# A decoder trunk with three token mixers: four Delta solutions planned side by side, with other ranks, waits, costs and priorities

## The chip, the core and the metric

The kernel runs on one core of a Trainium2 chip. The metric is the time of one execution on the device, in microseconds (us); of several runs the median counts. Four engines compute: TensorE (PE in the profile) multiplies matrices, VectorE (DVE) and ScalarE (ACT) work element by element, GpSimd (POOL) as well, and it also issues some of the transfers here; SyncE (SP) issues the others. Each engine works through its own queue in order and waits there for what its next instruction needs.

## What is computed

Two layers on 512 positions of width 1024. Each has one wide projection, three mixers side by side whose outputs are gated and merged, and a SwiGLU network:

```
for layer in range(DEPTH):
    h = rmsnorm(x, attn_norm[layer])
    proj = h @ w_in[layer]
    u_a, v_a, q_b, k_b, v_b, qkv_c, z_c, beta_c, a_c, gate_pre = split_columns(proj)
    out_a = spatial_gating(gelu(u_a), gelu(v_a), ...)
    out_b = sliding_window_attention(q_b, k_b, v_b, ...)
    out_c = gated_deltanet(qkv_c, z_c, beta_c, a_c, ...)
    merged = sum_i sigmoid(gate_i) * (out_i @ w_branch[layer, i])
    x = x + merged @ w_out[layer]
    gu = rmsnorm(x, ffn_norm[layer]) @ w_gate_up[layer]
    x = x + (silu(gu[..., :D_FF]) * gu[..., D_FF:]) @ w_down[layer]
return rmsnorm(x, final_norm)
```

The change concerns the gated DeltaNet, `out_c`, of four heads of width 128. Its core, in each chunk:

```
decay = exp(where(tril, gc[..., :, None] - gc[..., None, :], -inf))
lower = where(strict, (k_beta @ k^T) * decay, 0)
sol   = triangular_solve(lower + eye, [v * beta, k_beta * exp(gc)])
attn  = (q @ k^T) * decay
# then over the chunks, in order, with a state of 128 x 128 per head:
v_new = u_c - w_c @ state;  o_c = q_dec @ state + attn @ v_new
state = state * c_dec + k_dec^T @ v_new
```

## The kernel before

**Dense work.** All large products are made of 128x512 matmuls in three passes, each operand split into a high and a low part (`hH`, `hL`; `wh`, `wl`). A block of weights is loaded to `st`, rounded by ACT to `wh`, and DVE makes the rest `wl`; both carry a high priority. These matmuls write to four banks called `mm`.

**The Delta mixer.** The four heads form two groups (`Delta(gi)`) of two heads, and the 512 positions four chunks of 128 (`NCH`), so there are eight pairs of group and chunk. For each pair stand these steps, which share four banks called `px`: `decay` (a product of `gg`, the decays' logs, with a triangle; ACT's exponential; POOL's mask, into `la`), `keys` (transposes and squares of the keys, their norms on ACT and DVE, then `la[:, :, 0]`, written to memory as `blkscr`), `queries`, `values`, `solve` and `scan`. Once the keys of both groups are there, `blocks` inverts all diagonal blocks of 16x16 at once: POOL reads `blkscr` back as `nx`, DVE makes `tb` in 15 pairs of a product (`prd`) and a sum, POOL writes `tb` and its transpose to memory (`sc`) and reads them back as `cols`. Every `solve(c)` begins with `Tm` (DVE) and `Uc` (POOL) made from `cols`, and doubles the size of the block from 16 to 32, 64 and 128: PE makes a product, DVE or ACT evicts it as `ys`, PE makes the second, DVE subtracts it and transposes. `scan` goes through a group's chunks in order.

**The order of the work.** PE's order is fixed by a planner written by hand, `Issue`. Every stretch of work is a generator (a stream) with a rank, given by `spawn(rank, gen, after, slack)`. `run` takes the first ready stream in rank order up to its next `yield`; a lower rank goes first, and the dense work, rank 10 (`DENSE`), fills in when no other is due. A stream that yields a name waits until `set` of that name; one that yields a number is due at that time; a bare `yield` makes it due when all that it has just issued is done by the planner's reckoning (`issue.last`). `note` reckons these times with costs written in it, a latency `LAT` and so forth; they set PE's order only and are no times of the chip. On the other engines the framework's scheduler sets the order by its own reckoning and by the priorities given in the code (`tc.high_priority`).

The streams of a layer are these:

```
for e in d:
    issue.spawn(2, dn_stream(e))
    issue.spawn(3, e.solves())
    issue.spawn(1, qv_stream(e))
issue.spawn(4, keys_done())
```

Here `dn_stream` is decay and then keys, `qv_stream` queries, values and scan, `keys_done` blocks. Ranks 5 to 9 hold attention, the spatial gating and the branches' projections. The norm's stream has rank 0: `norm.finish()` starts from the time of its sums and a slack, 4.0 in layer 0, with four matmuls of `ones` and `sq` (the sums of squares), from which `rst`, the rows' scales, are made. `kv_out` then scales the keys and values of attention and the logits of beta and decay (`ba`), makes `gg` in a chain of small operations, and has PE sum it (`ex`).

The functions that the change touches and those that call them stand here with the line numbers of the profile (nearly all instructions are recorded under line 118, where the planner issues them, so they go by the names of their tiles):

Of the kernel before, what the change touches and what calls it, by code (L numbers as in the profile page):

```python
# [10 lines left out]
F32 = mybir.dt.float32  # L11
# [25 lines left out]
LAT = 0.7  # L37
DMA_LAT = 2.5
DENSE = 10
PAD = 48  # L40
ORDER = "k z qv0 qv1 aq gv u"
# [7 lines left out]
class Issue:  # L49
# [6 lines left out]
    def __init__(self):  # L56
        self.now = 0.0
        self.busy = {"vector": 0.0, "scalar": 0.0, "gpsimd": 0.0, "sync": 0.0}
        self.ready = {}
        self.read = {}  # L60
        self.banks = {}
        self.last = 0.0
        self.ahead = False
        self.events = {}
        self.streams = []

    def note(self, eng, op, args, kw):
        aps = [a for a in (*args, *kw.values()) if hasattr(a, "shape")]
        n = int(np.prod(aps[0].shape[1:]))
        dep = max((self.ready.get(a.tensor.name, 0.0) for a in aps), default=0.0)  # L70
        if eng == "tensor":
            m = int(np.prod(aps[1].shape[1:]))
            cost = n / 2400 if aps[1].dtype == F32R or op == "transpose" else max(4 * n, 4 * m) / 2400
            self.now = max(self.now, dep) + max(cost, m / 1200)
# [5 lines left out]
        else:  # L80
            if eng == "gpsimd":
                cost = 0.4 + n / 200 if ALU.pow in args else 0.1 + n / (430 if op == "tensor_tensor" else 900)
            else:
                cost = 0.07 + n / 960
            self.busy[eng] = max(self.busy[eng], self.now) + cost
            end = max(self.busy[eng], dep + cost) + LAT
# [4 lines left out]
        for a in [aps[0]] + ([kw["accum_out"]] if "accum_out" in kw else []):  # L91
            self.ready[a.tensor.name] = end
        self.last = max(self.last, end)
# [41 lines left out]
    def run(self):  # L135
        while self.streams:
# [12 lines left out]
            assert first is not None, [s[4] for s in self.streams]  # L149
            self.now = max(self.now, first[3])  # L150
# [12 lines left out]
def hybrid_kernel(ctx, tc, x0, pos, wi, wkv, wb, wo, wg, wd, gn, convw, lngb, sguw, sgub,  # L163
# [263 lines left out]
    def layer(l, norm, first=None):  # L427
        norm.after = f"kv{l}"
        issue.spawn(0, norm.finish(), norm.accs[0], 4.0 if l == 0 else 0.0)
# [35 lines left out]

        def kv_out():
# [3 lines left out]
            for c in range(NCH):  # L470
                r = rst[:, c:c + 1]
                nc.scalar.activation(kraw[:, c, :], banks[c][:, 0:128], AF.Copy, scale=r)
                nc.scalar.activation(vt[:, c, :], banks[c][:, 128:256], AF.Copy, scale=r)
                nc.vector.tensor_scalar(ba[:, c, :], banks[c][:, 256:264], r, None, ALU.mult)
            issue.set(f"kv{l}")
            nc.vector.tensor_scalar(rst8, rst, 0.125, None, ALU.mult)
            nc.vector.tensor_scalar(rsth, rst, 0.5, None, ALU.mult)

            def v44(t):
                return t.rearrange("p (c h) -> p c h", h=4)  # L480

            nc.vector.tensor_scalar(v44(bet), ba[:, :, 0:4], -1.0, 80.0, ALU.mult, ALU.min)
            nc.scalar.activation(bet, bet, AF.Exp)
            nc.vector.tensor_scalar(bet, bet, 1.0, None, ALU.add)
            nc.vector.reciprocal(bet, bet)
            sx = small("sx")
            nc.vector.tensor_tensor(v44(sx), ba[:, :, 4:8], db.unsqueeze(1).broadcast_to([P, NCH, 4]), ALU.add)
            se = small("se")
            nc.vector.scalar_tensor_tensor(se, sx, -1.0, sx, ALU.mult, ALU.min)
            nc.scalar.activation(se, se, AF.Exp)  # L490
            sz = small("sz")
            nc.vector.tensor_scalar(sz, se, 2.0, None, ALU.add)
            nc.vector.reciprocal(sz, sz)
            nc.vector.tensor_tensor(sz, sz, se, ALU.mult)
            sz2 = small("sz2")
            nc.vector.tensor_tensor(sz2, sz, sz, ALU.mult)
            spl = small("spl")
            nc.vector.tensor_scalar(spl, sz2, 1.0 / 17, None, ALU.mult)
            for kk in (15, 13, 11, 9, 7, 5, 3):
                nc.vector.scalar_tensor_tensor(spl, spl, 1.0 / kk, sz2, ALU.add, ALU.mult)  # L500

            nc.vector.scalar_tensor_tensor(spl, spl, 1.0, sz, ALU.add, ALU.mult)
            nc.vector.tensor_scalar(sx, sx, 0.0, None, ALU.max)
            nc.vector.scalar_tensor_tensor(spl, spl, 2.0, sx, ALU.mult, ALU.add)
            ea = small("ea", 4)
            nc.scalar.activation(ea, al, AF.Exp)
            nc.vector.tensor_scalar(ea, ea, -1.0, None, ALU.mult)
            nc.vector.tensor_tensor(v44(gg), v44(spl), ea.unsqueeze(1).broadcast_to([P, NCH, 4]), ALU.mult)
# [4 lines left out]
            nc.scalar.activation(ex, pgs[:, :48], AF.Exp)  # L513
            nc.vector.tensor_scalar(negc, egc, -1.0, None, ALU.mult)
# [36 lines left out]

        class Delta:
# [16 lines left out]
            def decay(self):  # L569

                for c in range(NCH):
                    col = self.col(c)
                    lg = self.wt([P, 2, P], "Tm", 2)
# [3 lines left out]
                    yield  # L577
# [4 lines left out]
                    nc.scalar.activation(la[:, :, 1, :], h2(ps), AF.Exp)  # L582
                    nc.gpsimd.tensor_tensor(la[:, :, 1, :], la[:, :, 1, :], bc(tri_le), ALU.mult)
                    self.la.append(la)
                    yield

            def keys(self):
# [4 lines left out]
                for c in range(NCH):  # L592
# [119 lines left out]
            def solves(self):  # L712
                for c in range(NCH):
                    if c >= 3:
                        yield f"o{l}{self.gi}{c - 3}"
# [656 lines left out]
```

## Time and profile before

| what | us |
|---|---|
| runs | 1751.05, 1754.48, 1752.0 |
| median | 1752.0 |
| the profiled execution | 1753.96 |
| its span, from the first to the last instruction | 1752.2 |
| PE busy / DVE / ACT / POOL | 1723.8 / 879.9 / 639.7 / 409.4 |

The mean granted clock of TensorE was 0.997 of its full rate. The profile names tiles as out<-in, so "mm<-hH,wh" is a dense matmul, "px<-Tm,la" the first product of a solution, "px<-ones,sq" one of the norm. Busy times of PE are modelled at the ends of the matmuls, so the distance from start to start tells more of its pace than the length of one. Mixers of layer 0 lie at some 30 to 300 us, those of layer 1 at some 900 to 1150 us; what lies between and after is the dense work of the branches and of the network.

### The profile page before, as it was taken

Reading aid. Unit: us, or ns where it says so; the run is one execution under the profiler, and the core shown is the slowest. Engines: PE = TensorE matmul, PEld = TensorE weight load, DVE = VectorE, ACT = ScalarE, POOL = GpSimd, SP = SyncE. Lnnn points to the kernel's source line nnn. Section 1 sums busy time; section 2 is a strip of 40 time slices with the busy share of each in tenths; the row PEclk is TensorE's granted clock in tenths of the full one; section 3 lists DMA queues with packets and bytes.
Section 4 is the critical chain, followed back from the end, with each engine's and each line's share of the span. In section 5 each row is a group of like instructions: output and inputs, shape, how many; then the busy total and the mean of one; then the engine's idle time right before and its main releaser. Section 6 shows DMA issues by size and latency. Waiting matters only on the chain.

```text
span 1752.2 us, 22016 instructions
## 1 busy us (share of the span) xinstructions
PE 1723.8 (98%) x8324; PEld 1424.9 (81%) x8324; DVE 879.9 (50%) x1744; ACT 639.7 (37%) x1180; POOL 409.4 (23%) x447
## 2 busy tenths in 40 slices
PE   9999899999999999999999999999999999999998
PEld 8888678888888888888888877788888888888886
DVE  7695775444543333323266958654445433333224
ACT  6454643322333222222244545533233322222212
POOL 2423221011223333310024142210212233333000
PEclk9999999999999999999999999999999999999999
DMA  5232102222352222234332220122223534444222
GB/s 165 87 106 85 37 25 90 85 93 100 102 181 96 97 96 97 96 107 134 121 121 87 97 73 25 55 85 97 96 86 131 162 120 121 120 121 156 97 97 84
DMA packets 73114, 176.57 MB, mean 101 GB/s; under 512 B 24944, under 2 KB 25200, under 8 KB 73008
## 3 DMA queue, kind: packets, MB, share of 16 engines
q1 hardware_dynamic: 71184, 170.71, 30.1%
q0 software_dynamic: 1248, 3.41, 0.7%
q8 instruction: 65, 1.06, 0.3%
q10 hardware_dynamic: 576, 1.05, 0.2%
q14 instruction: 41, 0.34, 0.1%
HBM read 162.03 MB, written 13.11 MB: 100 GB/s over the span
## 4 chain that ended last, share of the span: by engine, by line
PE 92%; DVE 4%; ACT 2%; POOL 1%; issue 1%; DMA 0%; SPq 0%; POOLq 0%; ACTq 0%; DVEq 0%
PE mm L118 81%; PE px L118 11%; ACT pr L118 1%; DVE pr L118 1%; DVE wl L118 0%; DVE U L118 0%; DVE zg L118 0%; POOL of L118 0%; DVE gw L118 0%; DMA x<-in_x 0%; ACT wh L118 0%; DVE gv L118 0%; DVE Tm L118 0%; DVE xf L118 0%; DVE ys L118 0%
## 5 line engine op out<-in xcount | busy, mean ns | idle before, releaser
L118 ACT CAST wh<-st 128x1024 fp32r<-128x1024 f32 (+2 forms) x286 | 295.9, 1035 | 829.5 <-PE mm L118 627.0
L118 PE MATMUL mm<-hH,wh 128*128 128x512 f32 x1344 | 532.5, 396 | 0.0
L118 PE MATMUL mm<-hH,wl 128*128 128x512 f32 x1344 | 523.8, 390 | 0.0
L118 PE MATMUL mm<-hL,wh 128*128 128x512 f32 x1344 | 523.2, 389 | 0.0
L118 DVE TENSOR_TENSOR wl<-st,wh 128x1024 fp32r<-128x1024 f32 (+2 forms) x286 | 352.5, 1232 | 222.1 <-ACT wh L118 211.4
L118 PEld LDWEIGHTS mm<-hH,wl 128*128 128x128 f32 x1344 | 252.2, 188 | 53.6
L118 PEld LDWEIGHTS mm<-hH,wh 128*128 128x128 f32 x1344 | 252.4, 188 | 53.3 <-issue 3.5
L118 PEld LDWEIGHTS mm<-hL,wh 128*128 128x128 f32 x1344 | 252.6, 188 | 50.9 <-issue 1.2
L118 POOL TENSOR_TENSOR s<-s,rep 128x512 f32<-128x512 f32 x44 | 77.6, 1763 | 162.0 <-ACT s L118 162.0
L118 POOL TENSOR_TENSOR aL<-s,aH 128x512 fp32r<-128x512 f32 x44 | 77.5, 1761 | 156.5 <-ACT aH L118 156.5
L118 POOL TENSOR_TENSOR gt<-gt,gt 128x512 f32<-128x512 f32 x32 | 48.8, 1524 | 272.6 <-DVE gt L118 272.6
L118 DVE TENSOR_TENSOR s<-mm,s 128x512 f32<-128x512 f32 x44 | 30.4, 692 | 143.9 <-PE mm L118 137.1
L118 DVE TENSOR_TENSOR s<-mm,rep 128x512 f32<-128x512 f32 x44 | 30.4, 691 | 138.3 <-PE mm L118 114.6
L118 DVE TENSOR_TENSOR gt<-mm,rep 128x512 f32<-128x512 f32 x48 | 33.1, 690 | 105.6 <-PE mm L118 105.6
L118 PE MATMUL mm<-wh,hH 128*128 128x512 f32 (+1 forms) x208 | 84.3, 406 | 1.2 <-ACT hH L118 1.2
L118 PE MATMUL mm<-wh,hL 128*128 128x512 f32 (+1 forms) x208 | 80.2, 385 | 0.6 <-DVE hL L118 0.6
L118 PE MATMUL mm<-wl,hH 128*128 128x512 f32 (+1 forms) x208 | 79.8, 384 | 0.0
L118 PE MATMUL mm<-brH,wh 128*128 128x512 f32 x192 | 74.7, 389 | 0.0
L118 PE MATMUL mm<-brL,wh 128*128 128x512 f32 x192 | 74.7, 389 | 0.0
L118 PE MATMUL mm<-brH,wl 128*128 128x512 f32 x192 | 74.7, 389 | 0.0
L118 PE MATMUL mm<-aH,wh 128*128 128x512 f32 x176 | 68.5, 389 | 0.0
L118 PE MATMUL mm<-aL,wh 128*128 128x512 f32 x176 | 68.5, 389 | 0.0
(285 smaller groups left out, 2510.9 us busy)
## 6 DMA issues: line engine op xcount, KB each, us to landing
st<-in_wi SPq DMA_DIRECT2D x104, 512.0 KB, 3.2
st<-in_wg SPq DMA_DIRECT2D x88, 512.0 KB, 3.3
st<-in_wb SPq DMA_DIRECT2D x24, 512.0 KB, 3.2
st<-in_wt SPq DMA_DIRECT2D x22, 512.0 KB, 3.2
st<-in_wo SPq DMA_DIRECT2D x16, 512.0 KB, 3.2
st<-in_wd SPq DMA_DIRECT2D x16, 512.0 KB, 3.6
xscr<-xt SPq DMA_DIRECT2D x24, 256.0 KB, 2.0
xt<-xscr SPq DMA_DIRECT2D x24, 256.0 KB, 2.9
```

The costliest lines, as they stand in the source:

```text
L118: return f(*args, **kw)
```

## The change

No instruction is added or removed; order, waits, priorities and buffers change.

- Planner: `LAT` 0.7 to 0.5; other costs in `note`, with the cost of a change between whole and partial tiles on PE; within `soon()` a result is reckoned from PE's own time.
- `soon()`, new: sets `issue.first` and a priority of 200 for what it encloses: the decays' exponential and mask, the keys' small operations and `la`, all of `blocks`, the evictions of `solve` and of the scan's states.
- `kv_out`: its operations stand under a high priority, in another order (the four on `ba` first, the chain of `gg` ahead of most else, ACT's scaling in the middle); `ea` is made ahead of it.
- Steps of decays, keys, queries and values yield `issue.bank_free("px", 4)` and `issue.now`: they wait for a free bank, no longer for their own last result.
- `solves(i)`: two streams per group, each with every second chunk; the wait of chunk 3 for the group's first output is gone. `scan` is a stream of its own; queries and values have rank 4.
- Buffers: `Tm`, `ys`, `Uc` 2 to 4 each, `U` 6 to 8. The norm's slack in layer 0: 4.0 to 1.0. The memory of the descriptors of dynamic transfers: set to 8192.

```diff
-LAT = 0.7
+LAT = 0.5
+SOON = 200
...
+                cost = (4 * max(n, m) + 24) / (4800 if tiled else 2400)
+            if tiled != self.tiled:
+                cost += 0.09
...
-            end = max(self.busy[eng], dep + cost) + LAT
+            end = max(self.now + cost, dep + cost) + 0.3 if self.first else max(self.busy[eng], dep + cost)
+            end += LAT
...
-        issue.spawn(0, norm.finish(), norm.accs[0], 4.0 if l == 0 else 0.0)
+        issue.spawn(0, norm.finish(), norm.accs[0], 1.0 if l == 0 else 0.0)
...
+        @contextmanager
+        def soon():
+            issue.first = True
+            with tc.high_priority(SOON):
+                yield
+            issue.first = False
...
-                    lg = self.wt([P, 2, P], "Tm", 2)
+                    lg = self.wt([P, 2, P], "Tm", 4)
...
-                    yield
+                    yield max(issue.last, issue.bank_free("px", 4))
...
                 for c in range(NCH):
+                    yield issue.bank_free("px", 4)
...
-                    yield
+                    yield issue.now
...
-                Tm, U = wt([P, 2, P], "Tm", 2), wt([P, 2, P], "Uc", 2)
+                with soon():
+                    Tm, U = wt([P, 2, P], "Tm", 4), wt([P, 2, P], "Uc", 4)
...
-            def solves(self):
-                for c in range(NCH):
-                    if c >= 3:
-                        yield f"o{l}{self.gi}{c - 3}"
-                    yield f"blocks{l}"
+            def solves(self, i):
+                yield f"blocks{l}"
+                for c in range(i, NCH, 2):
                     yield from self.solve(c)
 
             def scan(self):
                 yield f"z{l}"
+                yield f"qv{l}{self.gi}"
...
-            yield from e.scan()
+            issue.set(f"qv{l}{e.gi}")
...
             issue.spawn(2, dn_stream(e))
-            issue.spawn(3, e.solves())
-            issue.spawn(1, qv_stream(e))
+            for i in range(2):
+                issue.spawn(3 + i / 10, e.solves(i))
+            issue.spawn(4, qv_stream(e))
+            issue.spawn(1, e.scan())
...
-    nc = bacc.Bacc("TRN2", target_bir_lowering=False, num_devices=1)
+    nc = bacc.Bacc("TRN2", target_bir_lowering=False, num_devices=1, dynamic_dma_scratch_size=8192)
```

Three places of the order. First PE at the head of layer 0, where the norm's sums are multiplied (`px<-ones,sq`). Before, they stand among dense matmuls of the first wide tile (`mm_69`):

```order
L118 MATMUL mm_69_371<-hH_22_138,wh_71_373 128x512
L118 MATMUL mm_69_371<-hL_23_139,wh_71_373 128x512
L118 MATMUL mm_69_371<-hH_22_138,wl_72_374 128x512
L118 MATMUL px_73_399<-ones_78,sq_26_188 128x1 x4
L118 MATMUL mm_69_371<-hH_24_142,wh_71_373 128x512
L118 MATMUL mm_69_371<-hL_25_143,wh_71_373 128x512
```

In the change they stand inside the matmuls of 264 columns (`px_46`, `px_47`: keys and values of attention):

```order
L137 MATMUL px_46_246<-wh_16_117,hH_20_130 128x264
L137 MATMUL px_46_246<-wl_17_118,hH_20_130 128x264
L137 MATMUL px_46_246<-wh_16_117,hL_21_131 128x264
L137 MATMUL px_48_314<-ones_78,sq_26_188 128x1 x4
L137 MATMUL px_47_247<-wh_16_117,hH_18_126 128x264
L137 MATMUL px_47_247<-wl_17_118,hH_18_126 128x264
```

The norm's matmuls moved ahead, in front of the last tile of the narrow projection.

Second PE at the first solutions of layer 0 (`px<-Tm,la` is a solution's first product, `px<-ys,Uc` its second, `px<-kT,qT` attention). Before:

```order
L118 MATMUL mm_1681<-wl_1720,hH_112 128x512
L118 MATMUL mm_1681<-wh_1719,hL_113 128x512
L118 MATMUL px_1763<-Tm_1743,la_664 128x128 x2
L118 MATMUL px_1768<-Tm_1747,la_670 128x128 x2
L118 MATMUL px_1779<-kT_1220,qT_1741 128x128
L118 MATMUL px_1780<-kT_1220,qT_1741 128x128
...
L118 MATMUL px_1817<-ys_1766,Uc_1744 128x128 x2
L118 MATMUL px_1824<-ys_1771,Uc_1748 128x128 x2
```

In the change (`px<-dq,dk` are steps of queries):

```order
L137 MATMUL mm_1210<-hL_139,wh_1212 128x512
L137 MATMUL mm_1210<-hH_138,wl_1213 128x512
...
L137 MATMUL px_1266<-dq_1029,dk_384 128x128
L137 MATMUL px_1266<-dq_1120,dk_462 128x128
L137 MATMUL px_1278<-Tm_1235,la_535 128x128 x2
L137 MATMUL px_1283<-Tm_1239,la_547 128x128 x2
L137 MATMUL px_1288<-Tm_1243,la_562 128x128 x2
L137 MATMUL px_1293<-Tm_1247,la_574 128x128 x2
L137 MATMUL px_1298<-ys_1281,Uc_1236 128x128 x2
```

Four solutions, two of each group, now start together, and without attention between; in the program they come some 280 rows sooner on PE.

Third DVE at the end of `blocks` in layer 0 (`prd` and `tb` are its product and sum, `COPY` its transpose). Before:

```order
L118 TENSOR_REDUCE tb_1399<-prd_1402 128x14
L118 TENSOR_TENSOR prd_1402<-tb_1399,nx_1396 128x225
L118 TENSOR_REDUCE tb_1399<-prd_1402 128x15
L118 TENSOR_TENSOR wl_1684<-st_1682,wh_1683 128x1024
L118 COPY nx_1396<-tb_1399 128x256
L118 TENSOR_TENSOR Tm_1743<-cols_1434,blk_155 128x256
```

In the change (`pre`, `cv`, `dq` are steps of a convolution; `mm_1162` is the last tile of the first group's values):

```order
L137 TENSOR_REDUCE tb_903<-prd_906 128x14
L137 SCALAR_TENSOR_TENSOR dq_1120<-pre_1152,cv_1154 128x512
L137 TENSOR_TENSOR prd_906<-tb_903,nx_900 128x225
L137 TENSOR_TENSOR pre_1200<-mm_1162,rep_457 128x512
L137 TENSOR_TENSOR wl_1665<-st_1663,wh_1664 128x1024
L137 TENSOR_REDUCE tb_903<-prd_906 128x15
L137 SCALAR_TENSOR_TENSOR cv_1202<-pre_1200,cw_228,cv_1202 128x511
L137 COPY nx_900<-tb_903 128x256
```

Operations of the convolutions and of `wl` now stand between those of the blocks, one of which reads a tile that PE makes.

## Rows read from the trace of the kernel before

**Rows 1.** The page, busy times of the engines over the span, us and share.

```profile
PE 1723.8 (98%) x8324; PEld 1424.9 (81%) x8324; DVE 879.9 (50%) x1744; ACT 639.7 (37%) x1180; POOL 409.4 (23%) x447
```

**Rows 2.** Stretches: from and to, length; busy us (count) per engine; clock, DMA.

```profile
150.00:300.00 150.00, 140.87 (x850) 111.69 (x849) 100.37 (x343) 71.98 (x201) 42.84 (x79) 1.00 0.16 53
550.00:600.00 50.00, 50.00 (x222) 41.41 (x221) 17.25 (x18) 14.39 (x18) 16.14 (x10) 1.00 0.30 101
1000.00:1150.00 150.00, 141.66 (x864) 113.82 (x863) 102.63 (x360) 77.96 (x225) 44.15 (x77) 0.99 0.17 55
```

**Rows 3.** Waits of PE: for whom, us in total, times, longest.

```profile
PE px L118 <- DVE mxv L118: 4.3, 6, 1.2
PE px L118 <- ACT ys L118: 3.4, 3, 1.3
PE px L118 <- DVE rsum L118: 2.3, 1, 2.3
```

**Rows 4.** A stretch behind the wait for rsum; the clock is third from last.

```profile
1038.00:1040.00 2.00, 2.00 (x7) 1.63 (x7) 0.00 (x0) 0.37 (x1) 0.00 (x0) 0.50 0.00 0
```

**Rows 5.** Timeline of PE and DVE at the head: start, length, instruction, [idle before].

```profile
17.89 0.28 PE L118 MATMUL px<-wh,hH 128*128 128x264 f32 x1
18.94 0.68 DVE L118 TENSOR_TENSOR sq<-sq,sq 128x512 f32<-128x512 f32 x1
19.90 1.23 DVE L118 TENSOR_TENSOR wl<-st,wh 128x1024 fp32r<-128x1024 f32 x1 [0.28 <-ACT wh L118]
21.79 0.68 DVE L118 TENSOR_TENSOR sq<-sq,sq 128x512 f32<-128x512 f32 x1
...
48.93 0.37 PE L118 MATMUL px<-gg,tri_le 128*128 128x16 f32 x2 [0.86 <-DVE gg L118]
```

**Rows 6.** Timeline of POOL and DVE, the blocks of layer 0.

```profile
119.91 0.72 POOL L118 DMA_DIRECT2D blkscr<-la  x1 [2.90 <-DVE la L118]
...
127.49 0.29 DVE L118 TENSOR_SCALAR nx<-nx 128x256 f32<-128x256 f32 x1 [0.68 <-DMA nx<-blkscr]
...
141.35 0.39 DVE L118 TENSOR_REDUCE tb<-prd 128x15 f32<-128x225 f32 x1
141.66 1.22 DVE L118 TENSOR_TENSOR wl<-st,wh 128x1024 fp32r<-128x1024 f32 x1
142.04 0.57 POOL L118 DMA_DIRECT2D sc<-tb  x1 [17.43 <-DVE tb L118]
142.79 0.38 DVE L118 COPY nx<-tb 128x256 f32<-128x256 f32 x1
143.47 0.55 POOL L118 DMA_DIRECT2D sc<-nx  x1 [0.86 <-DVE nx L118]
...
147.16 1.16 POOL L118 DMA_DIRECT2D cols<-sc  x1 [1.46 <-DMA sc<-nx]
148.34 0.76 DVE L118 TENSOR_TENSOR Tm<-cols,blk 128x256 f32<-128x256 f32 x2 [5.17 <-DMA cols<-sc]
```

**Rows 7.** Timeline of DVE, the blocks of layer 1.

```profile
985.14 0.29 DVE L118 TENSOR_SCALAR nx<-nx 128x256 f32<-128x256 f32 x1 [1.17 <-DMA nx<-blkscr]
...
1006.17 0.38 DVE L118 TENSOR_REDUCE tb<-prd 128x15 f32<-128x225 f32 x1
```

**Rows 8.** Groups of instructions by form: busy us in all, mean ns of one.

```profile
L118 DVE TENSOR_TENSOR wl<-st,wh 128x1024 fp32r<-128x1024 f32 x270 | 339.2, 1256 | 209.2 <-ACT wh L118 198.6
...
L118 DVE SCALAR_TENSOR_TENSOR la<-px,sj,la 128x128 f32<-128x128 f32 x64 | 20.3, 343 | 0.0
...
L118 DVE SCALAR_TENSOR_TENSOR cv<-pre,cw,cv 128x511 f32<-128x511 f32 x24 | 18.0, 749 | 0.8 <-ACT cv L118 0.8
...
L118 POOL TENSOR_TENSOR Uc<-cols,blk 128x256 f32<-128x256 f32 x16 | 13.2, 840 | 16.8 <-PE px L118 11.5 <-DMA cols<-sc 5.3
```

**Rows 9.** Transfers issued by POOL: times, size, median us from issue to landing.

```profile
blkscr<-la POOLq DMA_DIRECT2D x16, 128.0 KB, 2.2
cols<-sc POOLq DMA_DIRECT2D x4, 128.0 KB, 3.8
```

More of the change, by code (lines that the diff above doesn't have):

```diff
@@ L56, in __init__ @@
     def __init__(self):
-        self.now = 0.0
+        self.now = self.idle = 0.0
+        self.tiled = False
         self.busy = {"vector": 0.0, "scalar": 0.0, "gpsimd": 0.0, "sync": 0.0}
         self.ready = {}
+        self.made = {}
         self.read = {}
@@ L62, in __init__ @@
         self.last = 0.0
-        self.ahead = False
+        self.ahead = self.first = False
         self.events = {}
@@ L69, in note @@
         n = int(np.prod(aps[0].shape[1:]))
-        dep = max((self.ready.get(a.tensor.name, 0.0) for a in aps), default=0.0)
+        dep = max((self.ready.get(a.tensor.name, 0.0) - (LAT if self.made.get(a.tensor.name) == eng else 0.0)
+                   for a in aps), default=0.0)
         if eng == "tensor":
-            m = int(np.prod(aps[1].shape[1:]))
-            cost = n / 2400 if aps[1].dtype == F32R or op == "transpose" else max(4 * n, 4 * m) / 2400
-            self.now = max(self.now, dep) + max(cost, m / 1200)
+            m, k = int(np.prod(aps[1].shape[1:])), aps[1].shape[0]
+            tiled = aps[1].dtype != F32R and (k < P or m < P)
+            if aps[1].dtype == F32R:
+                cost = (n + 32) / 2400
+            elif op == "transpose":
+                cost = (n + 132) / 2400
+            else:
+                cost = (4 * max(n, m) + 24) / (4800 if tiled else 2400)
+            if tiled != self.tiled:
+                cost += 0.09
+            self.tiled = tiled
+            self.idle += max(0.0, dep - self.now)
+            self.now = max(self.now, dep) + cost
             end = self.now
@@ L149, in run @@
             assert first is not None, [s[4] for s in self.streams]
+            self.idle += max(0.0, first[3] - self.now)
             self.now = max(self.now, first[3])
@@ L479, in v44 @@
[L479 to L488, printed above, removed]
@@ L499, in kv_out @@
[L499 to L507, printed above, removed]
@@ L659, in values @@
                                              scale=self.nk[c][:, hl:hl + 1])
-                    yield
+                    yield issue.now
             def solve(self, c):
@@ L690, in solve @@
                             nc.tensor.matmul(pz[:, hs(hl)], lhsT=ys[:, hl, :], rhs=U[:, hl, :], start=True, stop=True)
-                        nc.vector.tensor_tensor(U, U, h2(pz), ALU.subtract)
-                        for hl in range(2):
-                            nc.vector.transpose(Tm[32:64, hl, 0:32], U[0:32, hl, 32:64])
+                        with soon():
+                            nc.vector.tensor_tensor(U, U, h2(pz), ALU.subtract)
+                            for hl in range(2):
+                                nc.vector.transpose(Tm[32:64, hl, 0:32], U[0:32, hl, 32:64])
                     yield
@@ L739, in scan @@
                         nc.tensor.matmul(pY[:, hs(hl)], lhsT=U[:, hl, :], rhs=nv[hl], start=True, stop=True)
-                    y = la[:, :, 0, :]
-                    nc.scalar.copy(y, h2(pY))
+                    with soon():
+                        y = la[:, :, 0, :]
+                        nc.scalar.copy(y, h2(pY))
                     yield
```

214 lines of the change are left out of this document (123 added, 91 removed).

## The prediction, made before the changed kernel was run

> **What bounds the kernel now.** I read the busy times first: PE is busy for 1723.8 us of the span of 1752.2 us, and DVE, the next, for 879.9 us [rows 1]. No instruction is added or removed on any engine, so the time can only change by what PE waits. The 28 us in which PE is not busy are the whole stock, plus what the clock costs. Next I read stretches. In an undisturbed one PE starts 222 matmuls in 50 us, that is one dense matmul per 0.225 us [rows 2]. The two stretches in which the mixers' small matmuls run, 150 to 300 and 1000 to 1150 us, show 9.1 and 8.3 us without PE [rows 2]. A matmul's end is modelled, so part of a wait hides under the one before it: the wait for rsum, 2.3 us in the list of waits [rows 3], is 2.4 us from start to start. Adding up what each step in these stretches takes beyond the median of its kind gives **13.0 us** in layer 0 and **12.2 us** in layer 1; the difference to the 9.1 and 8.3 us is that hidden part. I use the larger numbers. They are scattered: mxv six times for 4.3 us in all, ys copied by ACT three times for 3.4 us, rsum once for 2.3 us [rows 3]. These releasers are results of DVE and ACT, not banks or buffers.
>
> The clock has a price of its own. After PE's wait for rsum, at 1036.7 us, the granted clock falls to 0.50, the lower level of 1.2 GHz, and PE starts 7 matmuls in 2 us [rows 4]. Of the 12.2 us, 1.7 us are matmuls at that level; I take 1.7 us as the price of each wait of such length.
>
> **Part 1, the waits of the mixers, taken away.** Four solutions side by side, later queries and values, and evictions ahead of the weights' splits on DVE and ACT (`soon`) are meant for these waits. In the order the solutions come in rounds of four pairs of matmuls, four times 0.45 us by 8 matmuls of 128 columns; the steps of the scan that follow have six dense matmuls, 1.35 us, between them; attention comes after the Delta work with far more dense work around it. At best all 25.2 us go. What is left: DVE needs 4 x 0.38 us for a round of ys (two operations of that size on Tm took 0.76 us [rows 6]), no more than PE's 1.8 us; the round that also transposes needs about 3.0 us, against 1.8 and some 0.7 us of dense work between, twice a layer; then ACT's copies. I take 2.0 us a layer, from ends of 0 and 5 us (three waits like before's for ACT's ys, 3.4 us, and one for mxv, 1.2 us [rows 3]).
>
> **Part 2, the head of layer 0.** The slack of `norm.finish` falls from 4.0 to 1.0, so the four matmuls of the norm move up by 51 matmuls. PE reached that place at 17.89 us; the last sum of squares ended at 21.79 + 0.68 = 22.5 us, behind a wl of 1.23 us at 19.90 us [rows 5]. In the new order on DVE this wl stands behind the sums and ACT makes the last square ahead of a cast: the add that ended at 18.94 + 0.68 = 19.6 us is followed by two of 0.68 us, so 21.0 us. PE waits 21.0 - 17.9 = **3.1 us** (4.6 us if nothing comes sooner on DVE, 1.9 us if the wl before the first add goes too). The decay's logs gg likewise move up, by 78 matmuls: PE would come there at about 32.8 us. The chain of some 21 small operations of 0.2 us on DVE, with a wl and the rotary steps ahead of it, ends by its new order at about 35.0 us: **2.2 us** (0 to 4), against 1.0 us before, start to start, ahead of the row at 48.93 us [rows 5]. In layer 1 nothing of either kind is late, as there the norm's sums lie under the last dense tiles. Sum of the head: 5.3 - 1.0 = +4.3 us. If the clock falls after the first wait, PE only comes later to the second.
>
> **Part 3, the blocks, which lose their cover.** All solutions start from `cols`, made by the longest chain of the kernel: the key products la go to memory, come back as nx, 15 pairs of product and sum on DVE make tb, tb and its transpose go to memory and return as cols. In the kernel before so much dense work stood ahead of the first solution that nothing waited for cols. In the changed order the first solution stands 165 matmuls behind the last key product: 153 dense at 0.225 us and 12 small at some 0.15 us, **36.2 us** of cover (36.1 us in layer 1). Against it stands:
>
> From the last key product to la: four key steps now stand in a row on PE (2.7 us), and each asks DVE for four small operations, two of la and two of kd, about 1.4 us back to back (la takes 0.34 us [rows 8], kd is of the same size, a small one 0.15 us). Four of them and a wl make 6.8 us, of which 1.1 us passes under PE's steps: 5.7 us. From the issue of la's write to the first operation on nx: 127.49 - 119.91 = 7.6 us [rows 6]. From there to the end of the last sum: 141.74 - 127.49 = 14.3 us in layer 0 and 1006.55 - 985.14 = 21.4 us in layer 1 [rows 6, 7], depending on what DVE does between. The new order puts 17 operations of about 512 columns between (six on zg, three pre, six cv, two dq), each taken as a cv, and four wl [rows 8]. A row starts about 0.08 us before the one ahead ends on record (141.66 + 1.22 against 142.79 us [rows 6]), so these are 17 x 0.67 + 4 x 1.18 = 16.1 us. The chain's own 30, of 0.15 us at first and 0.39 us for the last sum, add up to 8.0 us, of which 6.1 remain by the same overlap: 22.2 us, nearest to the 21.4 of layer 1. From the last sum to the first operation on cols: 148.34 - 141.74 = 6.6 us; the transposed half is copied after one more cv (1.0 us), its return is issued 147.16 - 143.17 = 4.0 us after that copy's end [rows 6] and lands 3.8 us later [rows 9], and POOL's Uc takes 0.84 us [rows 8]: 9.6 us.
>
> So Uc is there 5.7 + 7.6 + 22.2 + 9.6 = 45.1 us after the last key product; PE would use it at 36.2 + 1.8 = 38.0 us: 7.1 us late, and four Uc in a row at 0.84 us against pairs of 0.45 us add 1.2 us. **8 us** a layer, and 1.7 us for the clock. There is a floor under it: ahead of the last sum in DVE's queue stands pre of the values' last tile, which PE finishes only 5.9 us ahead of the first solution. The same working from there gives 2.0 + 9.6 - 7.7 + 1.2 = 5 us, even if DVE were early with all else. The chain before it has no wait for PE that is later than this.
>
> **Sum.** Against the profiled execution (1753.96 us; its span of 1752.2 lies 1.8 us below it, and it stands 0.1% above the median of 1752.0), the changed kernel waits 3.1 + 2.2 + 2 x (8 + 1.7 + 2.0) = 28.7 us where it waited 1.0 + 13.0 + 12.2 = 26.2 us: +2.5 us, **1754.5 us** from the median. Other parts are free: the constant ea moves to where ACT is idle; the costs of `note` are only the plan's; doubled buffers cost memory. The smaller descriptor memory has no row; I bound it below by nothing (it can't hasten an issue) and above by a wait of each of the four last writes of la for the landing of the one before it, 2.2 us [rows 9], some 6 us a layer, and take nothing.
>
> **Rivals.** (A) *The chain is at its floor and the solutions run clean.* DVE is ahead because four key steps come early, 5 us remain a layer, the clock doesn't fall, nothing is left of part 1, the head costs 1.9 us and no gg: 1.9 + 2 x 5 + 2 x 0.5 = 13 against 26.2 us, near 1740 us; with the head as forecast, 1742 us. For it speaks the 14.3 us of layer 0; against it the 21.4 us of layer 1 and the list of DVE's rows. (B) *Slower: POOL's part comes later.* The four writes of la, nx, sc and cols are issued by POOL in order between four powers for nk. If each issue stood behind one more operation or the landing of a write, some 5 to 6 us a layer would come on top: 1754.5 + 2 x 5.5 = 1765.5 us. It decides from the point where POOL reaches the last write of la after DVE made it. Against it: POOL is busy for 409.4 us in all [rows 1]. The Trainium skill ("SBUF — State Buffer", Who interferes with whom) says that a DVE instruction with two SBUF inputs, like a wl, and a GpSimd instruction that reads SBUF contend, the later one waiting for the other's end. In the trace the issue of sc at 142.04 us, which lay beside a wl, took 0.57 us, and the one at 143.47 us, with DVE idle, 0.55 us [rows 6]. For issues the rule does not show here; by it, four blocked steps of 1.26 us a layer would give 1754.5 + 2 x 5 = 1764.5 us. (C) *The change does not do what it says*: DVE stays the limit of the solutions (by its order it has some 65 us of work in 70 us of PE's), the old waits stay at 12.6 us a layer, and the new come on top: 5.3 + 2 x 22.3 - 26.2 = +23.7, 1776 us. (D) *All covered*: waits go, blocks are in time: 1752 - 26.2 + 4 = 1730 us.
>
> **How the numbers follow.** Forecast 0.45 (own range 1749 to 1760), A 0.23, B 0.20, C 0.05, D 0.07. The predicted time is the forecast's. The range 1740 to 1768 leaves out D, C and the outer ends of A and B, about 0.2. Faster and slower by 0.2% (3.5 us, about what a measurement of this kernel can tell from no change): faster is D and nearly all of A, 0.28; same is two thirds of the forecast and a little of A, 0.32; slower is B, C and the rest, 0.40.
>
> **What would show it.** After: a wait of PE of some 3 us near 18 us for sq; one for gg near 33 us; in each layer one wait of 5 to 9 us some 36 us after the last key product, released by DVE's Tm, POOL's Uc or the queries' operands, with a granted clock of 0.5 behind it; and few waits for mxv, rsum or ys beyond it. I am wrong if cols lands before PE asks (A, D), if the list of waits still holds those of before (C), or if POOL's issues stretch (B).

## The result, and the profile after

The changed kernel takes **1793.78 us** (median; 1793.25 to 1796.35), the kernel before in the same session 1753.07 us: a ratio of 1.0233, 95% interval 1.0220 to 1.0246. It is slower by 41 us where 1754.5 us had been forecast, and outside the range of 1740 to 1768 us.

The page's busy times, as in [rows 1]:

```profile
PE 1734.3 (97%) x8324; PEld 1433.7 (80%) x8324; DVE 892.9 (50%) x1744; ACT 638.1 (36%) x1180; POOL 414.8 (23%) x447
```

The span is 1791.9 us, 39.7 us longer than before. PE, with the same 8324 instructions, is busy for 10.5 us more: these are matmuls at the lower clock (the mean granted clock is 0.985; before it was 0.997). The other 39.7 - 10.5 = 29.2 us are more time without PE: 57.6 us where there were 28.4. The list of PE's waits, as in [rows 3], shows for what:

```profile
PE px L137 <- DVE Tm L137: 11.5, 2, 9.4
PE px L137 <- DVE kd L137: 10.9, 2, 5.8
PE px L137 <- POOL pr L137: 8.2, 6, 2.1
PE px L137 <- DVE dq L137: 5.6, 2, 5.0
PE px L137 <- DVE dv L137: 5.1, 2, 4.0
PE px L137 <- DVE pf L137: 3.3, 1, 3.3
```

None of the three names of [rows 3] is among them: mxv, ys and rsum no longer hold PE. In their place stand few and long waits. Here they are in PE's timeline: the norm (its wait is put down to pf, which stands in DVE's queue behind the last sum of squares), the decay behind four key steps, the first solution of layer 0, and one of attention:

```profile
21.07 1.02 PE L137 MATMUL px<-ones,sq 128*128 128x1 f32 x8 [3.29 <-DVE pf L137]
...
51.96 0.61 PE L137 MATMUL px<-dk 128*128 128x128 f32 x4
58.39 1.19 PE L137 MATMUL px<-tri_le,Tm 128*128 128x128 f32 x4 [5.82 <-DVE kd L137]
...
122.97 3.79 PE L137 MATMUL px<-Tm,la 128*128 128x128 f32 x16 [9.44 <-DVE Tm L137]
...
244.61 1.00 PE L137 MATMUL px<-ident,pr 128*128 128x128 f32 x4 [1.69 <-POOL pr L137]
```

Sixteen matmuls of the solutions at 122.97 us take 3.79 us, about twice what they need at full clock (in the kernel before, eight of them start within 0.90 us, from 216.56 us on). The stretches around it (columns as in [rows 2]) show why:

```profile
124.00:126.00 2.00, 2.00 (x11) 2.00 (x11) 1.26 (x4) 0.00 (x0) 2.00 (x4) 0.50 0.00 0
126.00:128.00 2.00, 2.00 (x12) 2.00 (x12) 1.14 (x3) 0.00 (x0) 0.63 (x2) 0.55 0.00 0
128.00:130.00 2.00, 2.00 (x20) 2.00 (x20) 1.83 (x9) 0.15 (x1) 2.00 (x4) 1.00 0.00 0
```

The chain of the blocks in layer 0, as in [rows 6], on POOL and DVE:

```profile
82.75 0.72 POOL L137 DMA_DIRECT2D blkscr<-la  x1 [1.64 <-DVE la L137]
...
91.26 0.29 DVE L137 TENSOR_SCALAR nx<-nx 128x256 f32<-128x256 f32 x1 [4.00 <-DMA nx<-blkscr]
...
114.16 0.38 DVE L137 TENSOR_REDUCE tb<-prd 128x15 f32<-128x225 f32 x1
...
122.49 1.96 DVE L137 TENSOR_TENSOR Tm<-cols,blk 128x256 f32<-128x256 f32 x4 [2.68 <-DMA cols<-sc]
```

The last key product ended at 76.1 us. la is written 6.6 us later, nx begins 8.5 us after that, the sums take 114.54 - 91.26 = 23.3 us, and cols comes 8.0 us later: 46.4 us to Tm, against 36.2 us of cover; the rest are the waits of 0.7 us for dq and 9.4 us for Tm.

### The profile page after: what moved, and what is told of

It is laid out like the page before. It is cut to its first block, busy times and chain, and to the rows that moved or that the text cites. A ratio compares the mean times of both kernels' runs of the same rounds, so it can differ in the third digit from the quotient of the medians.

```text
span 1791.9 us, 22052 instructions
## 1 busy us (share of the span) xinstructions
PE 1734.3 (97%) x8324; PEld 1433.7 (80%) x8324; DVE 892.9 (50%) x1744; ACT 638.1 (36%) x1180; POOL 414.8 (23%) x447
```

## Experiments

Each time is a median beside runs of the kernel before on the same chip (1753.3 to 1754.0 us); ratios carry their 95% interval, some 2 to 3 us to either side. The runs were made on five chips, and the kernel before differs between them by 0.7 us; times that lie nearer to each other than some 3 us are not told apart.

| run | what it is | us | ratio |
|---|---|---|---|
| a1_norm_late | changed, slack 4.0 | 1793.0 | 1.0225 (1.0210 to 1.0241) |
| a2_keys_own_wait | changed, keys wait as before | 1775.9 | 1.0130 (1.0114 to 1.0145) |
| a3_solve_later | changed, solutions told 10 us later | 1785.6 | 1.0187 (1.0165 to 1.0209) |
| c1_old_costs | changed, old costs | 1769.9 | 1.0091 (1.0075 to 1.0108) |
| c1k_slack_1 | the same, keys wait as before | 1752.3 | 0.9990 (0.9981 to 0.9999) |
| c1kn_old_costs_keys | the same, slack 4.0 | 1741.4 | 0.9933 (0.9917 to 0.9950) |
| e4_after_no_rule | changed, without one rule of the costs | 1767.8 | 1.0083 (1.0068 to 1.0098) |
| e2_mended | the same, keys as before, slack 4.0 | 1752.0 | 0.9986 (0.9977 to 0.9995) |
| f1_all_own_waits | the same, queries and values as before | 1751.9 | 0.9987 (0.9977 to 0.9996) |
| b1_costs_only | before, new costs | 1775.8 | 1.0129 (1.0111 to 1.0147) |
| e1_costs_no_rule | the same, without the rule | 1756.6 | 1.0016 (1.0006 to 1.0026) |
| b2_lat_only | before, LAT 0.5 | 1743.2 | 0.9937 (0.9923 to 0.9950) |
| c2_side_by_side | before, solutions side by side | 1744.5 | 0.9948 (0.9934 to 0.9963) |
| s1_priorities | before, priorities of `soon` | 1742.3 | 0.9937 (0.9922 to 0.9951) |
| d1_side_and_priorities | before, both | 1741.0 | 0.9925 (0.9913 to 0.9938) |
| d3_and_kv_out | the same, `kv_out` as changed | 1749.2 | 0.9969 (0.9958 to 0.9980) |
| e3_side_prio_lat | d1, LAT 0.5 | 1751.5 | 0.9988 (0.9978 to 0.9998) |
| f2_prio_lat | before, priorities, LAT 0.5 | 1743.8 | 0.9943 (0.9928 to 0.9957) |

### The new waits, one at a time

The norm's slack:

```diff
-        issue.spawn(0, norm.finish(), norm.accs[0], 1.0 if l == 0 else 0.0)
+        issue.spawn(0, norm.finish(), norm.accs[0], 4.0 if l == 0 else 0.0)
```

> The changed kernel with the norm's slack of layer 0 back at 4.0, so that PE comes to the norm's matmuls 24 matmuls later; all else as changed. In the changed kernel PE waited 3.45 us there and the clock was low behind it. Theory (each new wait costs its length and 1.7 us of clock, and gives them back when it goes): the wait falls to under 1 us, the time by 3 to 5 us, to some 1789 to 1791 us. Rival (a wait that goes is only handed on to the next place, as DVE is behind everywhere): under 1 us is gained, 1793 us or more.

1793.0 us, within the noise of the changed kernel. The wait fell only from 3.3 to 1.6 us in the list, as the new costs keep the norm early, and nothing clear of the noise was gained: the rival, as far as half of one wait can tell.

Keys wait for their own last result:

```diff
                 for c in range(NCH):
-                    yield issue.bank_free("px", 4)
                     tk = slice(c * P, (c + 1) * P)
...
-                    yield issue.now
+                    yield
```

> The changed kernel with the steps of keys alone as before: each waits for its own last result instead of a free bank, so key steps stand some 15 to 30 matmuls apart and not four in a row, and the decay's matmul no longer stands right behind the fourth. Theory (the four steps in a row hold all four px banks until DVE has read them, and the decay behind them waits for one: 5.98 us in layer 0 and 5.24 us in layer 1, and the clock 1.7 us each): these waits go, the time falls by 10 to 15 us, to 1779 to 1784 us, with the waits for blocks no shorter. Rival (handed on): the keys' results come later, the blocks' wait grows by as much, and the time stays within 3 us of 1794 us.

1775.9 us, 18 us less, more than the theory asked for. The page and the list of PE's waits:

```profile
PE 1730.0 (98%) x8324; PEld 1430.1 (81%) x8324; DVE 894.1 (50%) x1744; ACT 637.3 (36%) x1180; POOL 414.9 (23%) x447
...
PE px L137 <- DVE Tm L137: 14.2, 4, 9.5
PE px L137 <- POOL pr L137: 7.9, 6, 2.0
```

kd is gone from the list, and the wait for Tm stays. So the four key steps do hold the four banks, and a decay behind them waits until DVE has read the first. In the changed kernel the last read of it is this kd, and PE starts at 58.39 us:

```profile
57.91 0.33 DVE L137 TENSOR_SCALAR kd<-px,kds 128x128 f32<-128x128 f32 x1
```

10.9 us of waits for kd go, and PE's busy time falls by 4.3 us, with the clock; the rest of the 18 us are shorter waits behind them. kd is the one read of a key step that stands outside `soon()`: la of the first step was done at 55.29 us, and rows of the second, third and fourth step stand between it and kd. No run gave kd the priority too.

The same edit on the kernel with the old costs (c1 to c1k below) gives 17.7 us, but that is no second measurement of this wait: only 5.0 us of waits at the keys go there, and the rest comes from the plan behind them.

The solutions are told to be ready later:

```diff
+            issue.last += 10.0
             issue.set(f"blocks{l}")
```

> The changed kernel with the planner told that the blocks are ready 10 us later: 39 (layer 0) and 42 (layer 1) more dense matmuls, 8.9 and 9.5 us, between the last key product and the first solution. Theory (the blocks' chain is 8 to 10 us longer than its cover, a cost of its own): the waits at the first queries and solutions (0.8 + 9.6 us and 5.2 + 2.2 us) fall to under 2 us a layer, and with the clock some 17 to 20 us are gained: 1774 to 1778 us. Rival (DVE is behind as a whole, so more dense work ahead with its conversions and convolutions only makes the chain longer): half of the waits stays, and 1783 us or more.

1785.6 us (1782.6 to 1790.2, the widest spread of all): 8 us of the 17 to 20. The first solution no longer waits for Tm, but queries still wait 5.0 us for dq in layer 1, and the second products of layer 0 now 4.8 us for ys, values 3.2 us for dv: DVE, loaded with the convolutions' and blocks' rows, hands the wait on. The theory's size falls, the rival's half stands.

### Which part of the plan takes the cover

> The kernel before with the planner's new costs alone (LAT 0.5 and the refitted costs of note); streams, ranks, waits, priorities and buffers as before. Its plan has 191 instead of 238 matmuls between the last key product and the first solution in layer 0, 153 instead of 231 in layer 1. Theory (the loss comes from the steps that wait for banks alone and from solutions that are due too early; the costs act mostly through the latter): layer 0 stays covered, layer 1 waits some 5 to 8 us for blocks, and the time rises by 3 to 10 us, to 1756 to 1763 us. Rival (the tighter costs as such pull every reader too near its writer and make most of the loss): 1775 us or more.

```diff
-LAT = 0.7
+LAT = 0.5
...
-                cost = 0.07 + n / 960
+                cost = 0.15 + n / 960 if eng == "vector" else 0.16 + n / 1200 + (0.19 if "accum_out" in kw else 0.0)
```

(and the rest of `note` as in the change). 1775.8 us, the rival: the costs alone lose 22 us in a kernel without any of the new streams, waits or priorities. Its list begins

```profile
PE px L136 <- DVE Tm L136: 16.8, 3, 9.6
PE px L136 <- DVE inv L136: 4.1, 1, 4.1
PE px L136 <- DVE gg L136: 3.9, 1, 3.9
```

that is the blocks in both layers, the norm and the logs. The other way round:

> The changed kernel with the planner's old costs (LAT 0.7, note as before); streams, ranks, bank waits, priorities, buffers and the slack of 1.0 as changed. In its plan 232 matmuls (204 of them dense) stand between the last key product and the first solution in layer 0, 235 in layer 1, against 165 and 167; the norm comes 39 and gg 66 matmuls later; four key steps still stand in a row with a decay behind them. Theory (the tighter costs make the waits for blocks, norm; the bank wait is apart from them): waits for blocks under 2 us a layer, none for the norm, the wait for kd of some 5 us a layer stays; 1794 - 5 - 22 = 1765 to 1770 us. Rival (the streams and bank waits as such make half of the loss): over 1778 us.

1769.9 us, within the theory's bounds, 24 us below the changed kernel: with the old costs 232 matmuls stand ahead of the first solution, Tm is waited for 2.5 us in all, and the norm 0.9 us. That the number fits is in part luck. The waits at the keys, some 5 us a layer by the theory, are 5.0 us in both layers together (put down to sj and kd), and dv, which the theory does not name, leads the list with 11.1 us. Next the latency by itself:

> The kernel before with LAT 0.5 in place of 0.7 alone. Its plan has 210 matmuls between the last key product and the first solution in layer 0 and 199 in layer 1, between the 238 and 231 of before and the 191 and 153 of the new costs. Theory (a wait appears where cover falls under the blocks' chain, some 45 us or 200 dense matmuls): under 3 us of wait for blocks in layer 0 and 0 to 4 us in layer 1; 1752 to 1760 us. Rival (the latency as such is what makes the loss of the new costs): 1768 us or more.

1743.2 us. Both expectations missed; LAT 0.5 alone (one line) makes the kernel faster than before by 11 us. So on the kernel before it is not the latency that hurts. One term that does is new in `note`:

```diff
-        dep = max((self.ready.get(a.tensor.name, 0.0) - (LAT if self.made.get(a.tensor.name) == eng else 0.0)
-                   for a in aps), default=0.0)
+        dep = max((self.ready.get(a.tensor.name, 0.0) for a in aps), default=0.0)
```

It takes the latency off where an engine reads its own result. For the 30 operations of the blocks' chain the plan so loses 30 x 0.5 = 15 us, and PE is sent to the solutions that much sooner.

> The kernel before with the planner's new costs, but without the rule that takes the latency off for a result of the same engine. Its plan has 226 matmuls between the last key product and the first solution in layer 0 and 211 in layer 1, against 191 and 153 with the rule. Theory (the rule shortens the plan's blocks, 30 operations in a row on DVE, by 15, and so took the cover): the waits for Tm of 7 and 10 us go, 1741 to 1752 us. Rival (the refitted costs of single operations make the loss): 1765 us or more, with 1775.8 us for all costs.

1756.6 us, 19 us less than with the rule, though not quite within the theory's bounds: Tm is gone from the head of the list, la (6.8 us, first at the values) and mxv (5.2 us) stand there. This kernel also has LAT 0.5, which alone gave 1743.2 us; so the refitted costs of single operations lose some 13 us even without the rule.

> The changed kernel without that rule in note, all else as changed. In its plan 238 and 250 matmuls stand between the last key product and the first solution, against 165 and 167; four key steps still stand in a row with a decay behind them, and the norm's slack is 1.0. Theory: the waits for blocks (18 us and some 7 us of clock) go, those for kd stay: 1794 - 25 = 1766 to 1772 us. Rival (blocks later only hand the wait on, as with the solutions told 10 us later, 1785.6 us): 1780 us or more.

1767.8 us, 26 us less than the changed kernel, as the theory said. pr, which attention waits for, falls with it from 8.2 to 2.0 us in the list, though no expectation spoke of it; the waits at the keys (sj and kd) fall from 10.9 to 5.0 us. In their place la is waited for once, 8.7 us, ahead of the keys of attention:

```profile
108.47 0.38 PE L136 MATMUL px<-ident,dq 128*128 128x128 f32 x2
108.69 0.61 PE L136 MATMUL px<-dq,dk 128*128 128x128 f32 x4
120.02 1.09 PE L136 MATMUL px<-ident,kraw 128*128 128x128 f32 x4 [8.65 <-DVE la L136]
...
114.73 1.96 DVE L136 TENSOR_TENSOR Tm<-cols,blk 128x256 f32<-128x256 f32 x4 [3.69 <-DMA cols<-sc]
119.53 0.34 DVE L136 SCALAR_TENSOR_TENSOR la<-px,sj,la 128x128 f32<-128x128 f32 x1
```

The transposes of `kraw` read no la. It is the wait of the key steps over again: four steps of queries in a row, from 106.48 to 109.05 us, hold the four px banks, and the next taker waits until DVE has read the first (la). DVE is late with it because Tm stands ahead in its queue and waits 3.7 us for cols.

### Side by side, priorities, and what is left

> The kernel before with the four solutions side by side alone: two streams of solutions a group, queries and values at rank 4, scan a stream of its own, buffers of 4, 4, 4 and 8, descriptor memory 8192; costs, steps, priorities and the order up to the first solution as before. Theory (blocks are covered, and rounds of four give DVE and ACT time): the waits for ys, mxv and rsum of the mixers fall from 25 to some 10 us, 1738 to 1746 us. Rival (attention now comes without Delta work between and waits for POOL's pr, 5 us a layer as in the changed kernel, or DVE is full anyway): 1750 us or more.

1744.5 us, in the theory's bounds. Side by side, with streams, ranks and buffers as in the diff above, is a gain of 9 us if the plan before it stays.

> The kernel before with the priorities of soon alone (decays, keys, blocks, solutions' and scan's evictions ahead on DVE, ACT and POOL); PE's order is that of before, instruction for instruction. Theory (the order on DVE and ACT is not what costs): within 4 us of before, 1749 to 1757 us, with fewer waits for ys and Tm and more for weights or attention. Rival (the evictions pushed ahead delay convolutions and weights' splits, which is the loss of the changed kernel): 1762 us or more.

The edit is `with soon():` around the lines of the diff, without its effect on the plan. 1742.3 us, 11 us faster, which neither side expected: ys, released by ACT, is waited for 1.0 us in all (3.4 in [rows 3]), rsum no more.

> The kernel before with the two parts that each gained alone: the solutions side by side (with their streams, ranks and buffers) and the priorities of soon; costs, steps, kv_out and slack as before. Theory (PE's idle and slow time is a stock of some 26 us in the mixers and 6 at the head; the parts draw on the same waits and so add up in part): 1734 to 1740 us. Rival (independent parts, 9 and 11 us): 1733 us or less. Rival (the priorities make the same gain as the order): 1742 us or more.

**1741.0 us**, the lowest median of all, but only 1.3 us ahead of the priorities alone, with intervals that overlap, and between the theory and its second rival. That side by side adds anything to the priorities is not shown; most of what side by side gains alone (9 us) is not there on top of them.

> As the run with the old costs, and the keys' steps wait for their own last result and the norm's slack is 4.0, as before the change. What is left of the change are the solutions side by side, the bank waits of decays, queries and values, and the priorities. Theory: the wait for kd goes as well, 10 to 14 us below the run with old costs alone, 1752 to 1757 us; if side by side frees the old waits of 13 us a layer, 1740 to 1747 us. Rival (the later keys hand the wait on to the blocks): no faster than the run with old costs.

1741.4 us, in the lower bounds. The change without its costs, its keys' step and its slack is as good as d1, with the new order of `kv_out` and the other bank waits in it. Its list:

```profile
PE px L121 <- DVE dv L121: 3.3, 3, 2.1
PE px L121 <- POOL pr L121: 1.8, 1, 1.8
PE px L121 <- DVE ssq L121: 1.6, 1, 1.6
```

> The changed kernel with the old costs and the keys' steps waiting for their own last result, but the slack of 1.0: it divides the 28.5 us between the run with the old costs (1769.9 us) and the one that also has the slack of 4.0 (1741.4 us). Theory (the keys' steps and what stands behind them make it): 1742 to 1747 us. Rival (the early norm shifts the whole plan of layer 0): 1750 us or more.

1752.3 us, the rival: the slack of 1.0 costs 11 us here, though the norm itself is waited for by 0.8 us only. The plan behind it differs, and the largest single wait in it is 5.7 us, put down to ssq of the queries. It stands at 112.87 us, at the transposes of `kraw` behind four steps of queries in a row, as in e4: a wait for a px bank. So of the 28.5 us, 17.7 go with the keys' step and 10.9 with the slack, both for the most part through the plan behind them. On the changed kernel the same slack gained nothing (a1): these are no prices of the parts, but of the parts in one plan.

> As the run with side by side and priorities, and kv_out in the changed kernel's order under its high priority (ba first, the chain of gg ahead). Theory: the one wait for gg of 1.0 us in layer 0 goes, nothing else changes by much: 0 to 2 us faster. Rival (rotary and weights' operations pushed back at the head make PE wait there): 2 us slower or more.

1749.2 us, 8 us slower than d1: the rival's sign, but not its place. The wait for gg goes, and mxv and pr are waited for by 8.7 us together in attention, where d1 had 3.0 us. How `kv_out`'s order brings that about was not followed. It is no cost of its own: c1kn has the same `kv_out` and differs from this kernel only in the bank waits of decays, queries and values, and it takes 1741.4 us.

> The changed kernel without that rule, with keys' steps waiting for their own last result and the norm's slack of 4.0; solutions side by side, the other bank waits, priorities, kv_out, LAT 0.5 and the refitted costs of single operations stay. Theory (these three were the loss): as the run with the old costs, keys and slack (1741.4 us) or a little faster, 1736 to 1744 us. Rival (the bank waits of queries and values or kv_out also cost once the rest is tighter): 1748 us or more.

1752.0 us, the rival's number: undoing three edits takes the whole loss of 41 us away, but the 11 us that d1 and c1kn gain are not there. dv is waited for by 8.0 us, in layer 1.

> As the mended change, and the steps of queries and values wait for their own last result as well, as before. Theory (steps that wait for a bank alone come before their operand is there, since the planner knows nothing of the queue on DVE): the wait for dv falls from 8 to under 3 us and the time to 1740 to 1746 us. Rival (values are late because the priorities push their convolution back; the step's own wait changes nothing): 1750 us or more, with dv still waited for.

1751.9 us: dv is gone from the list, la (5.3 us, at a transpose of values in layer 0) and pT (4.0 us, of which 3.4 us stood in e2 too) lead it. The time stays, and the bank waits of queries and values are not what keeps the mended change from 1741 us. What e2 has and c1kn has not are planner's costs alone: LAT 0.5 and the refitted costs of single operations. In the rows of DVE both runs show one thing ahead of their largest wait: its queue stands idle in front of the first Tm until cols lands (4.5 us in e2, 6.2 us in f1), and the operations that PE waits for stand behind Tm. No run moved Tm alone.

> The kernel before with side by side, the priorities and LAT 0.5, three parts that each gained alone (9, 11 and 11 us). Theory (they draw on one stock of waits): 1736 to 1742 us. Rival (still partly independent): 1733 us or less. Rival (LAT 0.5 leaves 210 and 195 matmuls ahead of the solutions, too few once solutions come four at a time): 1745 us or more.

> The kernel before with the priorities of soon and LAT 0.5 alone (each alone gave 1742 to 1743 us), without side by side. Theory (LAT 0.5 clashes with four solutions at once, not with the priorities): 1732 to 1742 us. Rival (LAT 0.5 pulls readers too near under the priorities too): 1748 us or more.

1751.5 us with side by side (the last rival) and 1743.8 us without (between theory and rival). LAT 0.5 gains nothing more under the priorities, and costs 10 us on top of both, which is as much as e2 lies above c1kn. Which wait turns it there is open; the lists name dq, pre, ys with 2 to 3 us each.

## Why the prediction was wrong

**Right, with their sizes.** The old waits went, all three kinds. The norm: 3.1 us forecast, 3.3 us in the list (3.45 from start to start), at 21.07 us where 21.0 was worked out. The blocks: 8 us a layer forecast, 0.7 + 9.4 us in layer 0 and 5.0 + 2.1 + 0.4 us in layer 1, with a chain to Tm of 46.4 us where the same terms gave 42.1: 6.6 for 5.7, 8.5 for 7.6, 23.3 for 22.2, 8.0 for 6.6. e4 shows that this wait hangs on the plan's cover: with 238 matmuls ahead none for Tm is left. The rivals A, B, C and D all failed: cols never came early, POOL issued the chain's writes in 0.55 to 0.77 us each (0.55 us at 115.78 us, beside two cv on DVE, so no issue was blocked there), and the old waits did not stay. C came nearest with its 1776 us, but by a sum of old and new waits that the lists do not show.

**The step that failed: the sum has no term for the px banks.** The keys' steps in a row were costed as a delay of la alone (part 3), and all else as "Other parts are free". Who needs their banks next was not asked. The order shows it: behind the fourth key step of the first group stands the last decay, which needs a px bank, all four are held, and DVE frees the first only 6 us later: 5.8 us in layer 0 and 5.1 in layer 1, where the sum had nothing, and a2 takes 18 us off the time with them. The removed wait for the own last result was no free edit; it had kept the key steps apart.

The rows of the kernel before had shown such waits, and they were misread. "These releasers are results of DVE and ACT, not banks or buffers" does not hold for mxv, the first line of [rows 3]. None of the six matmuls that wait for it reads mxv. One of them, with DVE's row maxima of attention's scores, which read a px bank:

```profile
224.96 0.42 DVE L118 CUSTOM_DVE_ANT_0 pr<-px,amask 128x256 f32<-128x256 f32 x1
225.31 0.08 DVE L118 DVE_READ_ACCUMULATOR2_ANT mxv<- 128x1 f32 x1
...
225.53 0.68 PE L118 MATMUL px<-Tm,la 128*128 128x128 f32 x4 [0.71 <-DVE mxv L118]
```

Between the scores and this product PE fills two other px banks (223.42 and 224.19 us); the fourth after the first of the scores' banks is that bank again, so PE starts when DVE has read it.

**"Attention comes after the Delta work with far more dense work around it".** It does not where it counts: pr is waited for six times, 8.2 us, with no dense matmul between at 244.61 us. e4 brings it to 2.0 us, so most of it again hangs on the plan. Likewise dv, 5.1 us, had no term: with pr that is 6.7 us a layer, where 2.0 us had been taken for what is left of part 1.

**The gg term** was wrong the other way, 2.2 us forecast and no wait: DVE ended the chain at 34.4 us, where 35.0 had been worked out, and PE came at 35.0 instead of 32.8 us, behind its stretch at the lower clock. The prediction had named that ("PE only comes later to the second") and not subtracted it.

**The clock** was priced about rightly for one wait (1.7 us), but counted for two waits. It fell behind seven in the mixers (the two for kd, Tm and dv in layer 0, dq in layer 1, one for pr in each layer) and behind the norm's, against one, rsum's, before. PE's busy time rose by 10.5 us, 1.5 us for each fall more. In all: 57.6 us without PE instead of 28.4, where +2.5 us had been summed. The range was too narrow for the same reason: it was built on the sizes of known terms, and not on a term that is missing.

**The planner.** The prediction said that the costs of `note` "are only the plan's". They are, and alone they lose 22 us (b1), 19 us less without one rule (e1). The cover of 36.2 us, on which part 3 rested, was this rule's work; the prediction saw the effect and not the cause. The memory of the descriptors, taken at nothing, was not varied alone; the issue of the last write of la takes 0.72 us in both kernels.

## What to carry to other kernels

A planner's cost is right when the plan comes out with enough work ahead of each reader, not when one operation's cost is closer to its duration: a chain on an engine that also serves others takes as long as what is queued between, and a latency that was too large per operation stood for that queue (e1, e4). That is no rule for a single number: the smaller latency alone gained 11 us here (b2), and cost 10 us in another plan (e3). When a wait on an own result is relaxed to a wait on a resource, list who takes the resource next and when its last reader is through. Undo parts one at a time: here side by side, priorities and a shorter latency each gained 9 to 11 us alone, and together with the other edits they lost 41.

## What the hardware showed

Some small operations on DVE grew while POOL ran its masks on la (51.09 to 54.74 us of the changed kernel): the same operation on two columns of ss took 0.68 us there and 0.17 us behind it. Not all did: a reciprocal at 53.44 us and a product at 54.01 us took 0.17 and 0.15 us. The slow ones end where a mask ends, the first at 53.41 us, beside the second mask's end at 53.38 us.

```profile
51.09 3.65 POOL L137 TENSOR_TENSOR la<-la,tri_le 128x256 f32<-128x256 f32 x4
...
52.73 0.68 DVE L137 TENSOR_SCALAR ss<-ss 128x2 f32<-128x2 f32 x1
...
56.32 0.17 DVE L137 TENSOR_SCALAR ss<-ss 128x2 f32<-128x2 f32 x1
```

The Trainium skill ("SBUF — State Buffer", Who interferes with whom) has DVE and GpSimd share a pair of ports, with `tensor_scalar` among the operations that can take the pair; the rows of ss agree with it, though no run here varied it alone. The three slow operations (0.55 to 0.68 us, where their like take 0.15 to 0.17 us) add some 1.3 us to the queue that held the banks.

The clock did not fall behind every wait. Behind the 1.69 us at 244.61 us the stretches 244 to 246 and 246 to 248 us have 1.00; behind the 2.12 us at 262.37 us the stretch from 264 to 266 us has 0.58; behind the 2.06 us at 1009.23 us the stretches from 1008 to 1014 us have 1.00 again.
